# The output projection of attention: seven block products for each of three pairs of output blocks, with two sums of weight blocks formed by adding transfers

## The chip, the cores and the metric

The kernel runs on one core of a Trainium2 chip. The metric is the device time of one execution in microseconds (us); three runs of the kernel before gave 1672.11, 1672.30 and 1672.94, median 1672.3. The engines that matter here are PE (the matrix engine, with its weight loads PEld), DVE and ACT (the two elementwise engines), POOL (here: small scalings, a broadcast, and transfers of its own queue) and SP (which issues most transfers).

## The reference

A two-layer encoder on 512 tokens of width 1024. Each layer mixes tokens in three gated branches, projects the gated sum with `w_out`, adds it to the residual `x`, and then runs a gated convolutional feed-forward. The part that the change touches is `merged @ w_out` and the norm behind it:

```python
def gated_parallel_mixer(h, w_in, ...):
    ...
    merged = (gates[:, :, 0] * (y_na @ w_br_na)
              + gates[:, :, 1] * (y_mla @ w_br_mla)
              + gates[:, :, 2] * (y_gqa @ w_br_gqa))
    return merged @ w_out

def reference(x, ...):
    for l in range(DEPTH):
        h = rmsnorm(x, norm1_g[l])
        x = x + gated_parallel_mixer(h, ...)
        h = rmsnorm(x, norm2_g[l])
        x = x + conv_ffn(h, w_up[l], conv_w[l], conv_b[l], w_down[l])
    return rmsnorm(x, final_g)
```

## The kernel before, in words

Activations stand transposed: `x` is eight tiles of 128 channels by 512 tokens, and every projection takes weight blocks of 128x128 as the stationary operand and 512 (or 256) tokens as the moving one. All products are done in three passes: weight and activation are each split into a high and a low part (`split`, L195: ACT casts the high part at L198 or L201, DVE subtracts it from the source for the low part at L199 or L202), and `mm3` (L207) adds high x high, high x low, low x high.

Weights come in "specs" in one fixed list. For each, SP loads a `raw` tile (three buffers), ACT writes `whi` and DVE `wlo` (five buffers each), and `weights` (L186) hands them to the products. So a weight is split at the earliest when PE has done with the one five places before it. The order on PE and SP is that of the code (`manual_schedule`, L409); on DVE it is that of the code only inside the items named at L421, and elsewhere a scheduler picks one order when the kernel is built. Whatever the order, each engine runs its own list strictly in turn: a DVE instruction that waits holds up all behind it.

Near the end of attention `merge` (L793) forms `merged[m]` for eight output blocks and splits each into a pair of `mo` tiles. `do_out` (L929) then makes the eight output blocks: a group of four in two halves of the inner dimension, and four more of 24 matmuls each, 192 matmuls of 512 columns in all. As each block comes out (`evac`), DVE adds it to `x[k]`, and `norm_piece` splits `x[k]` times the gain into `hh`, `hl` and adds its square to `acc`.

`do_up` (L946) starts the feed-forward: a group of four output blocks, again in two halves (inner blocks 0 to 3, then 4 to 7; 48 matmuls each). After the second block of the first half PE transposes `acc` (L241), from which DVE, POOL, a transfer of the POOL queue and a POOL broadcast (L243 to L258) make `rb`, the inverse root mean square of each token. `conv` (L959) is the first to need `rb`: DVE multiplies each output by it into `u` (L962).

The feed-forward's last projection already uses seven products of half the tokens for a pair of output blocks instead of eight (`do_sum`, L1004, weight sums in `prepare_sum`, L168, activation sums in `operands`, L984): DVE adds four pairs of weight tiles per pair of output blocks, and `load_sum` (L153) loads their parts several products ahead. The group that follows it in layer 0 (`lat` of layer 1) has its `acc` transposed after the fourth block of its first half.

Of the kernel before, what the change touches and what calls it, by code (L numbers as in the profile page):

```python
# [17 lines left out]
P = 128  # L18
# [20 lines left out]
RAWB, WB, GZB, PRIO = 3, 3, 5, 300  # L39
NP, AHEAD, EVAC = (6, 5), (7, 7, 4, 7, 7, 7, 7), 400  # L40
F2 = 2 * NP[0]
# [22 lines left out]
class Trunk:  # L64
# [88 lines left out]
    def load_sum(self, j, unit):  # L153


        w = unit["np"] * P
        pool = self.fb if unit["part"] else self.fa
        for name in {0: ("V11", "V21", "V22"), 2: ("V12",)}.get(j, ()):
            m, e = unit["m"] + int(name[1]) - 1, int(name[2]) - 1
            if name in ("V11", "V22"):  # L160
                t = pool.tile([P, w], F32, tag="own", name="own", bufs=4)
# [4 lines left out]
            self.nc.sync.dma_start(unit[name].rearrange("p (i c) -> p i c", c=P), rows[e])  # L166

    def prepare_sum(self, hi, lo, j, unit):  # L168


        add, w = self.nc.vector.tensor_add, unit["np"] * P
        if j == 0:
            unit["S1"] = (self.fb if unit["part"] else self.fa).tile([P, w], F32, tag="s1", name="s1")
            unit["S2"], unit["S3"] = unit["S1"], unit["V21"]
            add(unit["S1"], unit["V21"], unit["V22"])
        elif j == 2:
            add(unit["S2"], unit["S1"], unit["V11"])
        elif j == 3:
            unit["S4"] = unit["V12"]
            add(unit["S4"], unit["S2"], unit["V12"])  # L180
        elif j == 5:
# [138 lines left out]
    def schedule(self, l):  # L320
# [33 lines left out]
        for part, ms in enumerate(((0, 2, 4, 6), (2, 4) if l == L - 1 else (2, 4, 6))):  # L354
            for m in ms:
                unit = {"w": d["w_down"][l], "m": m, "part": part, "np": NP[part], "r0": part * F2 * P}
                W["sum", part, m] = [("sum", j, unit) for j in range(7)]
# [23 lines left out]
        s += [("br", 2, 7)]  # L381
        s += ["out"] + [("out", m) for m in range(4, KD)]
        n = 2 * (F2 + 1)
# [4 lines left out]
    def run(self):  # L388
# [20 lines left out]
        with self.tc.manual_schedule(engines={mybir.EngineType.PE, mybir.EngineType.SP}):  # L409
# [3 lines left out]
            for self.l, (s, self.W) in enumerate(self.plans):  # L413
                self.pr = self.par[self.l]
                for item in s:
                    name, args = (item, ()) if isinstance(item, str) else (item[0], item[1:])
                    self.item = item
                    if name in ATTN:
                        with self.tc.high_priority(offset=ATTN_PRIO):
                            getattr(self, "do_" + name)(*args)  # L420
                    elif item == ("two", 0) or name == "sum" and args[0]:  # L421
                        with self.tc.manual_schedule(engines={mybir.EngineType.DVE}):
                            getattr(self, "do_" + name)(*args)
                    else:
                        getattr(self, "do_" + name)(*args)
# [367 lines left out]
    def merge(self, b, m, ps):  # L793
# [8 lines left out]
        if b == 2:  # L802
            if m == 0:
                self.gps_.close()
                self.ops, self.op = self.open("mo")
                self.mo = []
            pair = [self.op.tile([P, S], F32R, tag=f"{n}{m}", name="mo") for n in ("mh", "ml")]
            self.split(*pair, self.merged[m], 0.5)
            self.mo.append(pair)

# [117 lines left out]

    def do_out(self, m=None):  # L929
        g = self.pr[:, PC_G2:PC_G2 + 8]  # L930

        def evac(k, ps):
            if k == 0:
                self.norm_begin()
            self.nc.vector.tensor_add(self.x[k], self.x[k], ps)
            self.norm_piece(k, g)
        if m is None:
            self.banks(g=[2, 3, 4, 5], d=[6, 7, 0, 1])
            self.group(self.W["out"], self.mo, {(1, i): (lambda i=i: evac(i, self.gbank[i])) for i in range(4)})
        else:  # L940
            evac(m, self.dense(self.spec(), self.mo))
            if m == KD - 1:
                self.ops.close()
                self.mxs.close()
# [59 lines left out]
    def do_sum(self, part, m):  # L1004
# [8 lines left out]
        for j, (spec, (operand, b, x, sign)) in enumerate(zip(self.W["sum", part, m], steps)):  # L1013
            ps, fresh = banks[b], j in (0, 1, 2, 5)
            operand += part and operand > 0
            c = slice(operand * 256, operand * 256 + 256)
            for i, (wh, wl) in enumerate(self.weights(spec)):
# [3 lines left out]
                mm(ps, wl, hi, start=False, stop=i == n - 1, skip_group_check=True)  # L1021
            if part and j in (2,5):
                self.done(self.todo.pop(0))
            with self.tc.high_priority(offset=EVAC):
                if j < 6:
                    nc.vector.tensor_tensor(x, x, ps, ALU.add if sign > 0 else ALU.subtract)
                else:
                    both = x.rearrange("p (n c) -> p n c", c=256)
                    nc.vector.tensor_tensor(both, both, ps.rearrange("p (n c) -> p n c", n=1).to_broadcast([P, 2, 256]),
                                            ALU.subtract)  # L1030
        if part:
            self.todo += [m, m + 1]
            if m == KD - 2:
                self.done(m)
                self.done(m + 1)
        elif m == KD - 2:
# [4 lines left out]

    def done(self, k):
        if self.l == L - 1:
            self.acc = self.sumsq(self.const, self.x[k], self.acc, self.ntags)
# [4 lines left out]
        if k == KD - 1:  # L1049
            for i in range(KD):  # L1050
                self.acc = self.sumsq(self.const, self.x[i], self.acc, self.ntags)
            self.leave()

# [193 lines left out]
```

## Time and profile before

| what | us |
|---|---|
| median of three runs | 1672.3 |
| time of the profiled execution | 1673.28 |
| its span, first to last instruction | 1671.5 |
| PE busy (share of the span) | 1662.4 (99%) |
| DVE busy | 1270.6 (76%) |
| ACT busy | 895.6 (54%) |
| POOL busy | 50.8 (3%) |

The profiled execution is some 1 us longer than the median; 1.8 us of its time lie outside its span. A timeline row of the trace reads: start in us, duration in us, engine, line, operation, output<-input, shape, and in brackets how long the engine had stood idle before it and for what. Matmul durations overlap (each begins before the one ahead has drained), so the pace is read from the starts.

### The profile page before, as it was taken

The page shows a single profiled execution, that of the slowest core. Times are in us where ns is not written, and L with a number is a line of the kernel's source. Part 1 is how long each engine was busy: PE and PEld are TensorE (multiplying, and loading weights), DVE is VectorE, ACT ScalarE, POOL GpSimd, SP SyncE. Part 2 cuts the span into 40 slices and gives each one's busy share as a digit, 9 for nine tenths or more (in the row PEclk, how much of TensorE's full clock was granted, in tenths as well). Part 3 has the DMA queues.
Part 4 walks back from the last instruction along what each step waited for, and adds up shares of the span by engine and source line. Part 5 has one row for each costly group of instructions (what it writes and reads, how often), then busy time and mean ns, then how long its engine had stood idle before and what let it go on. Part 6 is the DMA issues. An engine that isn't in the chain of part 4 may idle for free.

```text
span 1671.5 us, 24066 instructions
## 1 busy us (share of the span) xinstructions
PE 1662.4 (99%) x9163; PEld 1405.3 (84%) x9163; DVE 1270.6 (76%) x2151; ACT 895.6 (54%) x1575; POOL 50.8 (3%) x107
## 2 busy tenths in 40 slices
PE   9999999999999999999999999999999999999998
PEld 7788888888888889888987888888888888898888
DVE  7777866787549888787977687668866588987886
ACT  7664545775436443445567544467744454434454
POOL 1110000000000000000011100000000000000000
PEclk9999999999999999999999999999999999999999
DMA  6233223222324333333233333322223333333322
GB/s 181 75 99 89 80 76 95 77 76 76 107 76 126 100 93 98 109 93 100 79 103 82 86 84 88 93 79 75 66 82 108 100 113 89 99 90 115 101 80 85
DMA packets 289667, 155.57 MB, mean 93 GB/s; under 512 B 9136, under 2 KB 285632, under 8 KB 289552
## 3 DMA queue, kind: packets, MB, share of 16 engines
q1 hardware_dynamic: 287008, 148.88, 31.3%
q0 software_dynamic: 2256, 4.83, 0.9%
q8 instruction: 72, 1.18, 0.3%
q14 instruction: 43, 0.35, 0.1%
q10 hardware_dynamic: 288, 0.33, 0.1%
HBM read 151.89 MB, written 2.10 MB: 92 GB/s over the span
## 4 chain that ended last, share of the span: by engine, by line
PE 92%; DVE 2%; ACT 1%; issue 0%; DMA 0%; ACTq 0%
PE ps_ring L212 12%; PE ps_ring L213 12%; PE ps_ring L214 12%; PE ps_d L214 11%; PE ps_d L212 11%; PE ps_d L213 11%; PE ps_d L1021 4%; PE ps_d L1020 4%; PE ps_d L1019 4%; PE ps_g L212 2%; PE ps_g L214 2%; PE ps_g L213 2%; PE ps_ring L293 2%; PE ps_ring L280 1%; PE ps_ring L762 1%; DVE wlo L199 1%
## 5 line engine op out<-in xcount | busy, mean ns | idle before, releaser
L198 ACT CAST whi<-raw 128x1024 fp32r<-128x1024 f32 (+5 forms) x342 | 293.7, 859 | 437.2 <-PE ps_ring L213 155.7
L199 DVE TENSOR_TENSOR wlo<-raw,whi 128x1024 fp32r<-128x1024 f32 (+5 forms) x340 | 335.5, 987 | 60.3 <-ACT whi L198 58.5
L214 PE MATMUL ps_d<-hh,wlo 128*128 128x512 f32 x685 | 266.7, 389 | 0.0
L212 PE MATMUL ps_d<-hh,whi 128*128 128x512 f32 x685 | 266.5, 389 | 0.0
L213 PE MATMUL ps_d<-hl,whi 128*128 128x512 f32 x685 | 266.5, 389 | 0.0
L212 PE MATMUL ps_ring<-hh,whi 128*128 128x512 f32 x600 | 235.3, 392 | 1.1 <-DVE nm L877 0.6
L214 PE MATMUL ps_ring<-hh,wlo 128*128 128x512 f32 x600 | 233.7, 390 | 0.0
L213 PE MATMUL ps_ring<-hl,whi 128*128 128x512 f32 x600 | 233.6, 389 | 0.0
L214 PEld LDWEIGHTS ps_d<-hh,wlo 128*128 128x128 f32 x685 | 128.6, 188 | 27.2 <-DVE wlo L199 0.6
L213 PEld LDWEIGHTS ps_d<-hl,whi 128*128 128x128 f32 x685 | 128.6, 188 | 26.8
L212 PEld LDWEIGHTS ps_d<-hh,whi 128*128 128x128 f32 x685 | 128.6, 188 | 26.5
L1021 PE MATMUL ps_d<-ft,wlo 128*128 128x256 f32 x511 | 144.6, 283 | 0.0
L1020 PE MATMUL ps_d<-ft,whi 128*128 128x256 f32 x511 | 144.6, 283 | 0.0
L1019 PE MATMUL ps_d<-ft,whi 128*128 128x256 f32 x511 | 144.6, 283 | 0.0
L212 PEld LDWEIGHTS ps_ring<-hh,whi 128*128 128x128 f32 x600 | 112.6, 188 | 25.4 <-DVE pt L734 0.9
L214 PEld LDWEIGHTS ps_ring<-hh,wlo 128*128 128x128 f32 x600 | 112.6, 188 | 23.7
L213 PEld LDWEIGHTS ps_ring<-hl,whi 128*128 128x128 f32 x600 | 112.7, 188 | 23.0
L1019 PEld LDWEIGHTS ps_d<-ft,whi 128*128 128x128 f32 x511 | 98.1, 192 | 0.2
L1020 PEld LDWEIGHTS ps_d<-ft,whi 128*128 128x128 f32 x511 | 98.1, 192 | 0.2
L1021 PEld LDWEIGHTS ps_d<-ft,wlo 128*128 128x128 f32 x511 | 98.1, 192 | 0.0
L205 DVE TENSOR_TENSOR gz<-ps_ring,rb 128x512 f32<-128x512 f32 x44 | 30.4, 690 | 77.0 <-PE ps_ring L214 77.0
L205 DVE TENSOR_TENSOR u<-ps_d,rb 128x512 f32<-128x512 f32 x80 | 54.9, 686 | 37.0 <-PE ps_d L214 36.7
(352 smaller groups left out, 3184.1 us busy)
## 6 DMA issues: line engine op xcount, KB each, us to landing
raw<-in_w_in_dram SPq DMA_DIRECT2D x86, 512.0 KB, 3.9
raw<-in_w_up_dram SPq DMA_DIRECT2D x80, 512.0 KB, 3.7
raw<-in_w_down_dram SPq DMA_DIRECT2D x18, 384.0 KB, 3.8
own<-in_w_down_dram SPq DMA_DIRECT2D x16, 384.0 KB, 4.9
raw<-in_w_in_dram SPq DMA_DIRECT2D x17, 256.0 KB, 3.0
raw<-in_w_br_mla_dram SPq DMA_DIRECT2D x16, 256.0 KB, 2.8
raw<-in_w_br_na_dram SPq DMA_DIRECT2D x16, 256.0 KB, 2.8
raw<-in_w_br_gqa_dram SPq DMA_DIRECT2D x16, 256.0 KB, 2.8
```

What stands on the lines that cost most here:

```text
L198: nc.scalar.copy(hi, src)
L199: nc.vector.tensor_sub(lo, src, r32(hi))
L205: self.nc.vector.tensor_tensor(out, a, b, ALU.mult)
L212: mm(ps, sh, mh, start=first and k == 0, stop=False)
L213: mm(ps, sh, ml, start=False, stop=False)
L214: mm(ps, sl, mh, start=False, stop=last and k == n - 1)
L280: self.nc.tensor.transpose(out[2 * u + i][:, c * 64:c * 64 + 64], block[q], self.idf[q, q])
L293: self.nc.tensor.matmul(out, st[a], mv[b], start=first and t == 0, stop=last and t == 2)
L762: nc.tensor.matmul(pq[:, qs], self.vs[p][:, ch, j, :], pm[:].rearrange("p (k c) -> p k c", c=P)[:, ks], start=i == 0 and m == 0, stop=i == ...
L1019: mm(ps, wh, hi, start=fresh and i == 0, stop=False, skip_group_check=True)
L1020: mm(ps, wh, lo, start=False, stop=False, skip_group_check=True)
L1021: mm(ps, wl, hi, start=False, stop=i == n - 1, skip_group_check=True)
```

## The change

`do_out` becomes one item. Output blocks 0 and 1 are made densely (four specs, 48 matmuls of 512 columns): both blocks over inner blocks 0 to 5 first, then both over 6 and 7. Blocks 2 to 7 are made as three pairs by `do_sum` with seven products of 4 inner pairs x 3 passes, 84 matmuls of 256 columns a pair.

- `merge` calls `mixed`, which splits `merged[m]` into a wider `mo` tile, and for each odd `m` also forms two sums of half-token blocks (four DVE operations of 256 columns) and splits them (two of 512 columns on ACT and on DVE). 
- `load_sum` loads the weight block V21 twice, and POOL's queue then adds V22 into the one copy and V11 into the other straight from DRAM (`accum_op=ALU.add`). These are S1 and S3, the second and the last of the seven weights. DVE adds only S2 and S4.
- The norm behind the projection: `done` (L1042 before) splits `x[k]` inside the following unit; the squares of all eight blocks are added to `acc` when the last block is done. In the last unit (blocks 6 and 7) of the projections that use it, the one of the feed-forward in layer 0 among them, the four `done` calls now stand at the second, fourth, sixth and seventh product.
- `do_up` transposes `acc` after the fourth block of the first half, where it was the second, and uses other PSUM banks.
- The items `out` and all `sum` of parts 1 and 2 now have DVE in the order of the code.

```diff
-NP, AHEAD, EVAC = (6, 5), (7, 7, 4, 7, 7, 7, 7), 400
+NP, AHEAD, EVAC = (6, 5, 4), (7, 7, 4, 7, 7, 7, 7), 400
...
+            unit["rows", name] = rows[e]
+        if j == 0 and unit["part"] == 2:
+            unit["S1"], unit["S3"] = self.mxt(f"ynl{self.owns // 2 % 2}"), unit["V21"]
+            view = lambda n: unit[n].rearrange("p (i c) -> p i c", c=P)
+            self.nc.sync.dma_start(view("S1"), unit["rows", "V21"])
+            for n, other in (("S1", "V22"), ("S3", "V11")):
+                self.nc.gpsimd.dma_start(view(n), unit["rows", other], accum_op=ALU.add)
...
-        W["out"] = halves(d["w_out"][l], [m * P for m in range(4)])
-        for m in range(4, KD):
-            W["out", m] = [(d["w_out"][l], 0, KD, m * P, P)]
+        W["out"] = [(d["w_out"][l], k0 * P, nk, m * P, P) for k0, nk in ((0, 6), (6, 2)) for m in (0, 1)]
...
-        s += ["out"] + [("out", m) for m in range(4, KD)]
+        s += ["out"] + [("sum", 2, m) for m in (2, 4, 6)]
...
-                    elif item == ("two", 0) or name == "sum" and args[0]:
+                    elif item in ("out", ("two", 0)) or name == "sum" and args[0]:
...
+    def mixed(self, m):
+        nc, (i, e) = self.nc, divmod(m, 2)
...
+        self.split(*part(e), self.merged[m], 0.5)
+        if e == 0:
+            return
+        (b0, b1), (b2, b3) = ((t[:, :256], t[:, 256:]) for t in self.merged[m - 1:m + 1])
+        a, t = self.mxt("ynl2"), self.mxt("ynl3")
+        nc.vector.tensor_sub(a[:, :256], b0, b1)
+        nc.vector.tensor_sub(a[:, 256:], b3, b1)
+        self.split(*part(2), a, 0.5)
+        nc.vector.scalar_tensor_tensor(t[:, :256], a[:, :256], -1.0, b3, ALU.mult, ALU.subtract)
+        nc.vector.scalar_tensor_tensor(t[:, 256:], t[:, :256], -1.0, b2, ALU.mult, ALU.subtract)
+        self.split(*part(3), t, 0.5)
...
-            self.banks(g=[2, 3, 4, 5], r=[6], d=[7, 0, 1, 2, 3, 4, 5, 6])
+            self.banks(g=[0, 1, 2, 3], r=[6], d=[7, 4, 5, 6, 0, 1, 2, 3])
...
-            self.group(self.W["up"], self.h, {(0, 1): lambda: (self.norm_sums(), self.norm_spread()), (1, 0): lambda: conv(0), (1, 1): lambda: conv(1),
+            self.group(self.W["up"], self.h, {(0, 3): lambda: (self.norm_sums(), self.norm_spread()), (1, 0): lambda: conv(0), (1, 1): lambda: conv(1),
...
-            if part and j in (2,5):
-                self.done(self.todo.pop(0))
+            if part and j in ((1, 3) if m == KD - 2 else (2, 5)):
+                self.done(self.todo.pop(0), part)
...
+            if part and m == KD - 2 and j > 4:
+                self.done(m + j - 5, part)
...
-    def done(self, k):
-        if self.l == L - 1:
+    def done(self, k, part=1):
+        if part == 2:
+            self.norm_split(k, self.pr[:, PC_G2:PC_G2 + 8])
+        elif self.l == L - 1:
```

Two places show what the change moves. The numbers behind the names tell one tile from the next. First PE in the first group of `do_up`, layer 0, before: `ps_g_4985` and `ps_g_4986` are the second and third output block, `ps_r` the transposed `acc`.

```order
L212 MATMUL ps_g_4985<-hh_4813,whi_4939 128x512
L213 MATMUL ps_g_4985<-hl_4814,whi_4939 128x512
L214 MATMUL ps_g_4985<-hh_4813,wlo_4940 128x512
L241 MATMUL ps_r_5024<-idf_78,acc_4740 128x128 x4
L212 MATMUL ps_g_4986<-hh_4736,whi_4990 128x512
L213 MATMUL ps_g_4986<-hl_4737,whi_4990 128x512
L214 MATMUL ps_g_4986<-hh_4736,wlo_4991 128x512
```

The same engine and place with the change (`ps_g_5238` is the fourth block, `ps_g_5235` the first):

```order
L232 MATMUL ps_g_5238<-hh_4976,wlo_5260 128x512
L230 MATMUL ps_g_5238<-hh_5031,whi_5259 128x512
L231 MATMUL ps_g_5238<-hl_5032,whi_5259 128x512
L232 MATMUL ps_g_5238<-hh_5031,wlo_5260 128x512
L259 MATMUL ps_r_5311<-idf_78,acc_5203 128x128 x4
L230 MATMUL ps_g_5235<-hh_5097,whi_5277 128x512
L231 MATMUL ps_g_5235<-hl_5098,whi_5277 128x512
```

The transposes moved back by two blocks, 24 matmuls: they stand between the two halves of the group now.

Second, DVE from the reduction of that transposed `acc` to the first weight behind the group (its `wlo` is 1024 wide: `wlo_5132` before), before the change. `u` is an output of the group times `rb`, `c` a step of the convolution; the 512-wide `wlo` are weights of the group's second half.

```order
L243 TENSOR_REDUCE ms_5029<-ps_r_5024 128x4
L199 TENSOR_TENSOR wlo_5041<-raw_5038,whi_5040 128x512
L199 TENSOR_TENSOR wlo_5059<-raw_5056,whi_5058 128x512
L199 TENSOR_TENSOR wlo_5077<-raw_5074,whi_5076 128x512
L205 TENSOR_TENSOR u_5092<-ps_g_4984,rb_5034 128x512
L199 TENSOR_TENSOR wlo_5101<-raw_5098,whi_5100 128x512
L966 SCALAR_TENSOR_TENSOR c_5094<-u_5092,x0_67,c_5094 128x511
L967 SCALAR_TENSOR_TENSOR c_5094<-u_5092,x0_67,c_5094 128x511
L205 TENSOR_TENSOR u_5116<-ps_g_4985,rb_5034 128x512
L199 TENSOR_TENSOR wlo_5132<-raw_5129,whi_5131 128x1024
```

With the change, the same stretch of DVE (`wlo_5383` is the first weight behind the group, `wlo_5407` the next):

```order
L261 TENSOR_REDUCE ms_5316<-ps_r_5311 128x4
L217 TENSOR_TENSOR wlo_5328<-raw_5325,whi_5327 128x512
L217 TENSOR_TENSOR wlo_5352<-raw_5349,whi_5351 128x512
L223 TENSOR_TENSOR u_5343<-ps_g_5235,rb_5321 128x512
L223 TENSOR_TENSOR u_5367<-ps_g_5236,rb_5321 128x512
L217 TENSOR_TENSOR wlo_5383<-raw_5380,whi_5382 128x1024
L994 SCALAR_TENSOR_TENSOR c_5345<-u_5343,x0_67,c_5345 128x511
L994 SCALAR_TENSOR_TENSOR c_5369<-u_5367,x0_67,c_5369 128x511
L995 SCALAR_TENSOR_TENSOR c_5345<-u_5343,x0_67,c_5345 128x511
L217 TENSOR_TENSOR wlo_5407<-raw_5404,whi_5406 128x1024
```

Two more of the group's 512-wide weights stand ahead of the reduction now, and between the first `u` and the first weight behind the group there is one instruction (the second `u`) where there were four; that weight still stands behind the first `u`. Layer 1 has the same order at both places.

More of the change, by code (lines that the diff above doesn't have):

```diff
@@ L160, in load_sum @@
             if name in ("V11", "V22"):
-                t = pool.tile([P, w], F32, tag="own", name="own", bufs=4)
+                t = self.own(unit["part"], w)
             else:
@@ L166, in load_sum, with sums, own @@
             self.nc.sync.dma_start(unit[name].rearrange("p (i c) -> p i c", c=P), rows[e])
+            unit["rows", name] = rows[e]
[5 more added lines that the diff above has]
+                self.nc.gpsimd.dma_start(view(n), unit["rows", other], accum_op=ALU.add)
+    def sums(self, part):
+        return self.fb if part else self.fa
+    def own(self, part, w):
+        if part < 2:
+            return self.sums(part).tile([P, w], F32, tag="own", name="own", bufs=4)
+        self.owns += 1
+        return self.mxt(f"ynh{self.owns % 4}")
     def prepare_sum(self, hi, lo, j, unit):
         add, w = self.nc.vector.tensor_add, unit["np"] * P
-        if j == 0:
-            unit["S1"] = (self.fb if unit["part"] else self.fa).tile([P, w], F32, tag="s1", name="s1")
+        loaded = unit["part"] == 2
+        if j == 0 and loaded:
+            unit["S2"] = unit["S1"]
+        elif j == 0:
+            unit["S1"] = self.sums(unit["part"]).tile([P, w], F32, tag="s1", name="s1")
             unit["S2"], unit["S3"] = unit["S1"], unit["V21"]
@@ L180, in prepare_sum @@
             add(unit["S4"], unit["S2"], unit["V12"])
-        elif j == 5:
+        elif j == 5 and not loaded:
             add(unit["S3"], unit["V11"], unit["V21"])
@@ L805, in merge @@
                 self.ops, self.op = self.open("mo")
[L806 to L809, printed above, removed]
+                self.ff, self.owns = [], 0
+            self.mixed(m)
+    def mixed(self, m):
+        nc, (i, e) = self.nc, divmod(m, 2)
+        if e == 0:
+            self.ff.append([self.op.tile([P, 8 * 256], F32R, tag=f"m{n}{i}", name="mo") for n in "hl"])
+        part = lambda a: [t[:, a * S:(a + 1) * S] for t in self.ff[i]]
+        self.split(*part(e), self.merged[m], 0.5)
+        if e == 0:
+            return
[7 more added lines that the diff above has]
+        self.split(*part(3), t, 0.5)
     def do_gq_open(self):
@@ L1014, in do_sum @@
             ps, fresh = banks[b], j in (0, 1, 2, 5)
-            operand += part and operand > 0
+            operand += part > 0 and operand > 0
             c = slice(operand * 256, operand * 256 + 256)
@@ L1051, in done @@
                 self.acc = self.sumsq(self.const, self.x[i], self.acc, self.ntags)
-            self.leave()
+            if part == 2:
+                self.ops.close()
+                self.mxs.close()
+            else:
+                self.leave()
     def leave(self):
```

36 lines of the change are left out of this document (15 added, 21 removed).

## Prediction

> **What bounds the kernel now.** First the page's head, engine shares and chain of waits:
>
> ```profile
> span 1671.5 us, 24066 instructions
> PE 1662.4 (99%) x9163; PEld 1405.3 (84%) x9163; DVE 1270.6 (76%) x2151; ACT 895.6 (54%) x1575; POOL 50.8 (3%) x107
> PE 92%; DVE 2%; ACT 1%; issue 0%; DMA 0%; ACTq 0%
> ```
>
> PE holds 99% of the span and 92% of the chain. So what the change saves in PE time counts in full, and every wait it puts in front of PE counts in full too. Next the table by windows: the kernel's first 8 us, the last merges of layer 0, its output projection, and a stretch of seven-product units. Behind the window stand busy time and count of PE, PEld, DVE, ACT, POOL, then the granted clock, the DMA share and GB/s.
>
> ```profile
> 0.00:8.00 8.00, 6.54 (x26) 5.38 (x26) 3.04 (x10) 3.75 (x6) 0.40 (x5) 1.00 0.75 237
> 395.00:437.50 42.50, 42.50 (x189) 35.13 (x189) 26.49 (x42) 16.66 (x26) 0.00 (x0) 1.00 0.31 87
> 437.50:481.00 43.50, 43.50 (x194) 36.02 (x192) 25.54 (x36) 18.46 (x28) 0.00 (x0) 1.00 0.37 103
> 623.00:683.00 60.00, 60.00 (x501) 59.92 (x500) 51.47 (x75) 25.04 (x30) 0.00 (x0) 1.00 0.31 86
> ```
>
> PE never stands still in the stage that is rewritten, at full clock; DVE works 26.5 of 42.5 us before it and 25.5 of 43.5 in it. The timeline of PE gives the pace, and the places I need later:
>
> ```profile
> 1.04 3.35 PE L412 MATMUL idle<-early 128*128 128x128 f32 x14 [1.04 <-DVE cst L89]
> ...
> 437.70 0.39 PE L212 MATMUL ps_g<-mo,whi 128*128 128x512 f32 x1
> ...
> 481.00 0.39 PE L214 MATMUL ps_d<-mo,wlo 128*128 128x512 f32 x1
> 481.23 0.39 PE L212 MATMUL ps_g<-hh,whi 128*128 128x512 f32 x1
> ...
> 486.67 0.60 PE L241 MATMUL ps_r<-idf,acc 128*128 128x128 f32 x4
> ...
> 503.45 0.39 PE L212 MATMUL ps_d<-hh,whi 128*128 128x512 f32 x1
> 503.68 0.39 PE L213 MATMUL ps_d<-hl,whi 128*128 128x512 f32 x1
> 503.95 0.50 PE L214 MATMUL ps_d<-hh,wlo 128*128 128x512 f32 x1
> 504.29 0.39 PE L212 MATMUL ps_d<-hh,whi 128*128 128x512 f32 x1
> ...
> 623.31 0.28 PE L1019 MATMUL ps_d<-ft,whi 128*128 128x256 f32 x1
> ...
> 683.78 0.40 PE L212 MATMUL ps_d<-hh,whi 128*128 128x512 f32 x1
> ```
>
> The projection's 192 matmuls of 512 columns run from 437.70 to 481.23: 0.2267 us each. Four units of 126 matmuls of 256 columns run from 623.31 to 683.78: 0.1200 us each, a little over half.
>
> **The change, part by part.**
>
> *PE work.* Per layer 192 x 0.2267 = 43.5 us become 48 x 0.2267 + 252 x 0.1200 = 10.9 + 30.2 = 41.1 us: 2.4 us saved, 4.8 in two layers. The trace holds both paces side by side, so this term is firm. The Trainium skill ("TensorE: Matmul & The Clock Gate", section on the back-to-back issue gap) has 518 cycles at 2.4 GHz for 512 columns and 262 for 256, an estimate of 0.216 and 0.109 us; with those the saving would be 144 x 0.216 - 252 x 0.109 = 3.6 us a layer, 7.3 in all. The rows have a relatively dearer 256-column matmul, and the rows decide.
>
> *The norm behind the projection.* This is where I expect the saving to go. The timelines of DVE and POOL from the transposes of `acc` on, with the same `u` in layer 1 and the transposes ahead of it:
>
> ```profile
> 487.31 0.69 DVE L243 TENSOR_REDUCE ms<-ps_r 128x4 f32<-128x512 f32 x1 [2.04 <-PE ps_r L241]
> ...
> 499.05 0.69 DVE L205 TENSOR_TENSOR u<-ps_g,rb 128x512 f32<-128x512 f32 x1 [5.16 <-POOL rb L258]
> ...
> 502.08 0.68 DVE L205 TENSOR_TENSOR u<-ps_g,rb 128x512 f32<-128x512 f32 x1
> 502.68 1.21 DVE L199 TENSOR_TENSOR wlo<-raw,whi 128x1024 fp32r<-128x1024 f32 x1
> ```
>
> ```profile
> 490.25 0.74 POOL L257 DMA_DIRECT2D row<-rt  x1 [0.45 <-POOL rt L248]
> 497.81 1.21 POOL L258 PARTITION_BROADCAST rb<-row  x1 [6.81 <-issue]
> ```
>
> ```profile
> 1313.41 0.60 PE L241 MATMUL ps_r<-idf,acc 128*128 128x128 f32 x4
> ...
> 1325.77 0.69 DVE L205 TENSOR_TENSOR u<-ps_g,rb 128x512 f32<-128x512 f32 x1 [5.14 <-POOL rb L258]
> ```
>
> From the transposes to the first `u` it is 12.38 us in layer 0 and 12.36 in layer 1, most of it between POOL's transfer and its broadcast. Call the transposes' start T. Before, T comes 5.44 us after the group's start (486.67 - 481.23), the group ends 22.22 us after its start (503.45), and the first weight behind it is ready just in time: its subtraction starts at 502.68, and the matmul that needs it at 503.95, 0.05 late and with 0.11 us lost to the restart (504.29 - 503.95 = 0.34 in place of 0.23).
>
> With the change T lies 48 x 0.2267 = 10.88 us after the start. PE then needs 0.46 us for the transposes and 48 matmuls for the second half, and reaches the first matmul with the next weight's low part at T + 0.46 + 10.88 + 0.45 = T + 11.79. DVE's order has both `u` ahead of that weight: first `u` at T + 12.38, second 0.60 later (502.68 - 502.08), the subtraction at T + 13.58, the matmul 1.27 us after that (503.95 - 502.68), T + 14.85. PE waits 3.06 us, and pays 0.11 for the restart; 0.16 of that it paid before. Loss: 3.0 us a layer, 6.0 in all. Behind the waiting `u` on DVE stand this weight and all later ones. The next weight, after three steps of `c` of about 0.7, is done some 3.3 us after the first and is needed 5.4 us after it, so I count one wait a layer.
>
> *Is `acc` itself in time?* PE runs in order, so a late `acc` would delay it directly. The end of the feed-forward in layer 0 has the same pattern already (last unit, eight squares, transposes after the fourth block), on DVE and PE:
>
> ```profile
> 833.33 0.69 DVE L1029 TENSOR_TENSOR x<-x,ps_d 128x512 f32<-128x512 f32 x1 [0.53 <-PE ps_d L1021]
> 833.93 0.75 DVE L202 SCALAR_TENSOR_TENSOR hl<-x,par,hh 128x512 fp32r<-128x512 f32 x1
> 834.59 0.68 DVE L199 TENSOR_TENSOR wlo<-raw,whi 128x512 fp32r<-128x512 f32 x1
> ...
> 839.95 2.27 DVE L231 TENSOR_TENSOR acc<-acc,sq 128x512 f32<-128x512 f32 x3
> ```
>
> ```profile
> 844.04 0.60 PE L241 MATMUL ps_r<-idf,acc 128*128 128x128 f32 x4
> ```
>
> There `acc` is done at 842.2, 1.8 us before PE asks. The change has one more weight split ahead of the last addition, 0.6 us: 1.2 us of cover. I count nothing.
>
> *DVE in the seven-product units.* A unit of 84 matmuls lasts 10.08 us on PE. The evacuations of 256 columns on DVE's timeline, each with the row behind it:
>
> ```profile
> 797.61 0.41 DVE L1026 TENSOR_TENSOR x<-x,ps_d 128x256 f32<-128x256 f32 x1
> 797.94 0.82 DVE L180 TENSOR_TENSOR raw<-s,raw 128x640 f32<-128x640 f32 x1
> ...
> 799.41 0.41 DVE L1026 TENSOR_TENSOR x<-x,ps_d 128x256 f32<-128x256 f32 x1
> 799.81 0.83 DVE L199 TENSOR_TENSOR wlo<-raw,whi 128x640 fp32r<-128x640 f32 x1
> ```
>
> They take 0.33 and 0.40, mean 0.36. DVE does 7 weight splits and 2 additions of 512 columns (0.60 each by the spacing of the two rows at 502), six such evacuations and one of 512, and two norm splits of 0.66 (834.59 - 833.93): 5.4 + 2.2 + 0.6 + 1.3 = 9.5 us. With the two additions that the transfers take over it would be 10.7, more than PE. In the last unit, with three norm splits, it is 10.2; the five weight buffers carry 0.1 us. Nothing counted; 0.5 us a unit, 3 in all, as the other end.
>
> *The half-token sums in* `mixed`*.* Per pair of blocks four DVE operations of 256 and two of 512, 4 x 0.33 + 2 x 0.60 = 2.5 us. Three pairs fall among the last merges, where DVE stood idle for 16 us, and one at the projection's head, where it stood idle for 18 us of the whole; ACT is idle longer still. Hidden; without that cover it would be 2.5 us a pair.
>
> *The adding transfers.* No row before shows one. The nearest are in the listing of transfers by line, with size and median time to landing, and on SP's timeline:
>
> ```profile
> own<-in_w_down_dram SPq DMA_DIRECT2D x16, 384.0 KB, 4.9
> raw<-in_w_out_dram SPq DMA_DIRECT2D x16, 256.0 KB, 2.8
> rope<-in_rope_dram POOLq DMA_DIRECT2D x6, 256.0 KB, 3.4
> rope<-in_rope_dram SPq DMA_DIRECT2D x2, 256.0 KB, 7.0
> ```
>
> ```profile
> 804.68 0.53 SPq L166 DMA_DIRECT2D own<-in_w_down_dram  x1
> ```
>
> The low end is 3.4 us (the same queue and bytes, without adding), the high end 7.0 (twice the data, or the slowest transfer of this size); I take 3.4, the same queue. What hides it: the third pair's tiles can be loaded when DVE has split the first pair's S3, by an estimate from the five buffers when PE is at that pair's sixth product. From there to the third pair's second product it is ten products of 1.44 us, less 1.3 for the two steps of its own split: 13.1 us. The way is 3 x 0.5 (issues on SP) + 4.9 (loads, queued behind each other) + 2 x 0.74 (POOL's issues, by its row above) + 3.4 = 11.3, or 14.9 by the high end: 1.8 us of cover, or 1.8 late. The first pair's tile waits for a raw buffer that comes free with the last merge but one, 2.7 us before the projection begins, and is needed 12.3 us into it: about the same. DVE stands in turn behind a late S1, and PE behind it. Nothing counted; 1.8 us at each of two places, 3.6 a layer, 7.2 in all, as the other end. A gain from these transfers beyond the additions they replace is excluded, since PE waits for no such sum here.
>
> **The sum.** -4.8 + 6.0 = +1.2 us. The profiled execution's 1673.28 would become 1674.5; on the median of the runs, 1672.3, it is 1673.5. A measurement of this kernel can tell about 0.2%, 3.3 us, from no change.
>
> **The rivals.**
>
> *The saving arrives whole* (faster): the chain from T to `rb` shortens, or the next weight's split is not behind it. Then 1672.3 - 4.8 = 1667.5. Against it: two layers agree on the chain within 0.02 us, and DVE's order is fixed. Chance 0.09.
>
> *The adding transfers land late* (slower). Place: the splits of S1 in the first and third pair. It decides once a transfer takes more than 5.2 us from its issue (3.4 + 1.8). At the high end of 7.0 it costs 7.2 us, and the time is 1673.5 + 7.2 = 1680.7. For it: nothing in the trace bounds an adding transfer. Against it: SP's queue moves the same pieces of this weight in 2.8 us. Chance 0.12, half of it below 1678.
>
> *PE comes back slow after the wait* (slower). If it ran at half pace for as long as it had stood still, 3.1 us a layer, 6.2 in all: 1679.7. The same page of the Trainium skill (its part on the clock gate) says that PE falls to half its clock after an idle window of about 3.4 us. No row here shows a fallen clock: the longest wait in the timeline above is the 1.04 us at the start, and the first 8 us show 1.00. The forecast's wait is just under the page's window. Chance 0.07.
>
> *DVE becomes the bound in the units, or* `acc` *is late*: up to 3 us in all, 1674 to 1677. Chance 0.10.
>
> **How the numbers follow.** The forecast, one wait of 2.5 to 3.5 us a layer, 1672.5 to 1674.5, has 0.62, and the likeliest time is 1673.5. The range takes in the late `acc`, the transfers up to 5 us of their 7.2, and the case of a full DVE, 1671.0 to 1678.5; left out are the whole saving (0.09) and the far slower ends (about 0.09). Faster than 1669.0 is the first rival, 0.09; slower than 1675.6 are the late transfers (0.12), the slow PE (0.07) and half of the last case (0.05), 0.24; the rest, 0.67, is no measurable change.
>
> **What would show it.** Right: the profile after has PE idle about 3 us, at the third matmul of the first block behind the group of `do_up`, once a layer, put down to DVE's `wlo` behind `u` behind POOL's `rb`; the three units take 10.1 us each with no idle time on PE. Wrong: no such wait, or waits at the second product of a unit put down to a transfer on POOL's queue, or units longer than 10.3 us with DVE full.

## The result, and the profile after

The changed kernel takes 1691.7 us (median of four executions, 1688.9 to 1693.5), the kernel before 1672.3 beside it: a ratio of 1.0114, 95% interval 1.0097 to 1.0132. It is slower by 19 us, where 1.2 was forecast and 1678.5 was the range's upper end. The profiled execution took 1688.92 us, the shortest of the four; the other three had a mean granted clock of 0.994 or 0.995, this one 0.996, so what follows accounts for the shortest of them. Its page has, in answer to the three lines of before:

```profile
span 1687.1 us, 24783 instructions
PE 1666.2 (99%) x9379; PEld 1416.9 (84%) x9379; DVE 1315.8 (78%) x2267; ACT 915.3 (54%) x1617; POOL 68.3 (4%) x119
PE 65%; DVE 1%; issue 1%; DMA 1%; ACT 0%; POOLq 0%; POOL 0%; SPq 0%; ACTq 0%
```

PE still shows 99%, and is busy for longer although it has less to do: busy time says little where the clock falls. The chain of waits is no better guide here: PE's share of the span in it fell from 92% to 65%, but the chain, followed back from the end, stops at 507.84 us, at the first `u`, where before it went back to 63.51; the two shares cover different stretches. To see where the 15.6 us of span went, cut both traces at the same four instructions: first matmul of the projection, first of the feed-forward's group, the same two in layer 1, and the end. The columns are those of the table by windows (third from the end: the granted clock). Before:

```profile
437.70:481.23 43.53, 43.53 (x194) 36.04 (x193) 25.54 (x36) 18.29 (x29) 0.00 (x0) 1.00 0.37 103
481.23:1264.44 783.21, 782.10 (x4366) 662.49 (x4365) 606.75 (x1028) 424.54 (x749) 24.68 (x49) 1.00 0.32 91
1264.44:1307.96 43.52, 43.52 (x193) 36.05 (x192) 25.54 (x36) 18.28 (x29) 0.00 (x0) 1.00 0.36 103
1307.96:1671.50 363.54, 358.38 (x1975) 313.25 (x1973) 290.64 (x427) 173.34 (x237) 3.58 (x4) 1.00 0.33 98
```

After:

```profile
436.64:484.59 47.95, 44.17 (x302) 41.12 (x300) 35.70 (x68) 22.44 (x39) 7.79 (x6) 0.96 0.59 124
484.59:1272.17 787.58, 783.86 (x4368) 663.70 (x4366) 619.59 (x1055) 430.11 (x760) 24.71 (x49) 1.00 0.33 91
1272.17:1318.33 46.16, 43.63 (x302) 39.93 (x300) 35.34 (x68) 22.56 (x39) 7.78 (x6) 1.00 0.62 129
1318.33:1687.10 368.77, 360.02 (x1976) 314.32 (x1974) 295.54 (x435) 175.78 (x242) 3.56 (x4) 0.99 0.34 99
```

The two projections grew by 4.4 and 2.6 us, where 2.4 less was reckoned for each; the two stretches behind them grew by 4.4 and 5.2, where 3.0 was reckoned. (The sum is 16.7; 1.1 comes back because the first projection began 1.1 us earlier here.) What PE waited for, in us in all, times and the longest:

```profile
PE ps_d L232 <- DVE wlo L217: 5.7, 2, 2.9
PE ps_d L1047 <- ACT whi L216: 4.8, 3, 2.6
PE ps_d L1049 <- DVE wlo L217: 1.1, 5, 0.2
```

The first row is the forecast's wait for `rb`, once a layer. DVE's timeline in layer 0 has its cause, `u` waiting for `rb` and the weight standing behind both `u`:

```profile
507.86 1.29 DVE L223 TENSOR_TENSOR u<-ps_g,rb 128x512 f32<-128x512 f32 x2 [7.86 <-POOL rb L276]
509.07 1.22 DVE L217 TENSOR_TENSOR wlo<-raw,whi 128x1024 fp32r<-128x1024 f32 x1
```

The second is the one that the forecast named as the sign of its being wrong: PE stands ahead of a unit's second product, whose weight is S1. PE's timeline at the first pair of layer 0:

```profile
448.83 0.28 PE L1049 MATMUL ps_d<-mo,wlo 128*128 128x256 f32 x1
451.73 0.39 PE L1047 MATMUL ps_d<-mo,whi 128*128 128x256 f32 x1 [2.62 <-ACT whi L216]
...
452.92 0.41 PE L1049 MATMUL ps_d<-mo,wlo 128*128 128x256 f32 x1
453.13 0.41 PE L1047 MATMUL ps_d<-mo,whi 128*128 128x256 f32 x1
```

Behind the wait the matmuls start 0.21 us apart in place of 0.12. The table by windows shows why, around this wait and around the one for `rb` in both layers:

```profile
448.80:452.90 4.10, 1.25 (x8) 0.84 (x7) 1.19 (x2) 1.84 (x4) 1.28 (x1) 1.00 0.10 11
452.90:456.40 3.50, 3.50 (x19) 3.50 (x18) 3.50 (x8) 2.70 (x5) 0.16 (x1) 0.51 0.60 75
...
507.00:510.40 3.40, 0.52 (x4) 0.10 (x2) 2.54 (x4) 1.81 (x3) 0.83 (x1) 1.00 0.00 0
510.40:514.50 4.10, 4.10 (x11) 3.24 (x12) 4.10 (x6) 1.95 (x3) 0.00 (x0) 0.58 0.44 128
...
1344.10:1347.70 3.60, 3.60 (x10) 2.83 (x11) 3.60 (x6) 1.59 (x2) 0.00 (x0) 0.57 0.50 146
```

The granted clock is half for some 3.5 us behind each wait of 2.6 us or more, and it is 1.00 behind the one of 1.5 us at S1 in layer 1. Why S1 is late, from the timelines of POOL and ACT and the listing of transfers (the last number is the median time to landing):

```profile
439.63 1.39 POOL L172 DMA_DIRECT2D raw<-in_w_out_dram  x1 [238.54 <-DMA ynh<-in_w_out_dram]
445.13 1.29 POOL L172 DMA_DIRECT2D ynl<-in_w_out_dram  x1 [4.11 <-DMA raw<-in_w_out_dram]
451.29 1.28 POOL L172 DMA_DIRECT2D raw<-in_w_out_dram  x1 [4.87 <-issue]
456.24 1.27 POOL L172 DMA_DIRECT2D ynl<-in_w_out_dram  x1 [3.67 <-issue]
```

```profile
451.06 0.62 ACT L216 CAST whi<-ynl 128x512 fp32r<-128x512 f32 x1 [5.62 <-DMA ynl<-in_w_out_dram]
```

```profile
raw<-in_w_out_dram POOLq DMA_DIRECT2D x6, 256.0 KB, 4.6
ynl<-in_w_out_dram POOLq DMA_DIRECT2D x6, 256.0 KB, 5.4
```

POOL issues S3's adding transfer (into `raw`) ahead of S1's (into `ynl`) in every pair, although the code lists S1 first; an issue takes 1.3 us, and where the next stands ready it goes out 4.7 to 6.2 us after the one ahead, mostly with nothing to wait for that the profile shows ("issue"). The first pair's S1 came out at 445.13, its sum was there at 451.06, and PE had needed the split weight by about 448.95.

### The profile page after: what moved, and what is told of

Same layout as the page of the kernel before. It is cut to its first block, busy times and chain, and to the rows that moved or that the text cites. A ratio compares the mean times of both kernels' runs of the same rounds, so it can differ in the third digit from the quotient of the medians.

```text
span 1687.1 us, 24783 instructions
## 1 busy us (share of the span) xinstructions
PE 1666.2 (99%) x9379; PEld 1416.9 (84%) x9379; DVE 1315.8 (78%) x2267; ACT 915.3 (54%) x1617; POOL 68.3 (4%) x119
## 4 chain that ended last, share of the span: by engine, by line
PE 65%; DVE 1%; issue 1%; DMA 1%; ACT 0%; POOLq 0%; POOL 0%; SPq 0%; ACTq 0%
PE ps_d L232 10%; PE ps_d L231 10%; PE ps_d L230 10%; PE ps_ring L230 6%; PE ps_ring L231 6%; PE ps_ring L232 6%; PE ps_d L1049 4%; PE ps_d L1048 4%; PE ps_d L1047 4%; DMA ynl<-in_w_out_dram 1%; PE ps_ring L311 1%; PE ps_g L230 1%; PE ps_g L232 1%; PE ps_g L231 1%; PE ps_ring L298 1%
## 5 line engine op out<-in xcount | busy, mean ns | idle before, releaser
L216 ACT CAST whi<-raw 128x1024 fp32r<-128x1024 f32 (+4 forms) x344 | 291.2, 847 | 402.1 <-PE ps_ring L231 140.0
L217 DVE TENSOR_TENSOR wlo<-raw,whi 128x1024 fp32r<-128x1024 f32 (+4 forms) x342 | 331.6, 970 | 40.9 <-ACT whi L216 39.5
```

The source lines that it names most:

```text
L216: nc.scalar.copy(hi, src)
L217: nc.vector.tensor_sub(lo, src, r32(hi))
```

## The experiments

The theory: three losses, S1 late because of the adding transfers, the wait for `rb`, and half the clock behind each long wait. The rivals: another cause for the slow stretches, DVE full in the units, or transfers that are slow wherever they stand. Beside all of these kernels the kernel before took 1672.1 to 1672.3 us (and 1672.9 in the one execution beside the two probes of POOL).

### The weights behind the group ahead of `u` on DVE

```diff
+            with self.tc.manual_schedule(engines={mybir.EngineType.DVE}):
+                self.group(self.W["up"], self.h, {(0, 3): ..., (1, 3): lambda: conv(0)})
+            conv(1, 2, 3)
```

> The changed kernel, but in the first group of the feed-forward DVE splits both weights behind the group ahead of the first u, so that no weight stands behind rb. Theory (the wait for rb of 2.9 us a layer, and behind it some 3.5 us in which PE is granted about half its clock, 1.6 to 1.9 us lost each time): both go, 2 x (3.0 + 1.7) = 9.4 us less than the changed kernel's 1691.7, so 1682. Rival A (the slow stretch has another cause than the wait, such as the transfers of that time): only the waits go, 1685.7. Rival B (the next thing that depends on rb, a PSUM bank or the third weight behind the group, is late in its turn): 1688 to 1692.

1683.1 us (1681.2 to 1684.2), ratio 1.0065 (1.0051 to 1.0079): 8.6 less than the changed kernel. DVE's timeline now has both weights ahead of `u`, and PE no wait there and full clock:

```profile
502.26 1.23 DVE L217 TENSOR_TENSOR wlo<-raw,whi 128x1024 fp32r<-128x1024 f32 x1 [2.46 <-ACT whi L216]
504.98 1.23 DVE L217 TENSOR_TENSOR wlo<-raw,whi 128x1024 fp32r<-128x1024 f32 x1 [1.49 <-ACT whi L216]
507.58 1.29 DVE L223 TENSOR_TENSOR u<-ps_g,rb 128x512 f32<-128x512 f32 x2 [1.37 <-POOL rb L276]
```

```profile
502.00:510.00 8.00, 8.00 (x37) 6.63 (x36) 4.87 (x6) 3.86 (x5) 1.22 (x1) 1.00 0.57 166
```

`rb` is as late as ever and nobody waits for it but `u`. The loss was a matter of one queue's order, and the slow stretch went with the wait: rivals A and B fall.

### The transposes alone, in the kernel before

```diff
-{(0, 1): lambda: (self.norm_sums(), self.norm_spread()), ...
+{(0, 3): lambda: (self.norm_sums(), self.norm_spread()), ...
```

> The kernel before, with one edit: the transposes of acc after the fourth block of the first half instead of the second. The dense projection stays, and no adding transfer is in it. Theory: the wait for rb and the slow stretch behind it appear here too, 2 x (3.0 + 1.7) = 9.4 us over 1672.3, so 1681.7, with a granted clock of 0.5 to 0.6 for some 3.5 us behind each wait. Rival A (the clock falls for another reason, in the new units or their transfers): 1672.3 + 6.0 = 1678.3 with the clock at 1.00.

1682.2 us, ratio 1.0055 (1.0040 to 1.0070): as the theory had it, without one new unit or adding transfer. The slow stretch is not in every execution to the same amount: the four took 1683.9, 1683.3, 1681.2 and 1679.2 us, at mean granted clocks of 0.996, 0.996, 0.997 and 0.999. The profile is of the longest. Behind the waits:

```profile
507.20:512.00 4.80, 4.58 (x13) 3.63 (x14) 4.80 (x8) 2.65 (x3) 0.00 (x0) 0.64 0.42 122
...
1338.50:1345.50 7.00, 7.00 (x19) 5.51 (x20) 7.00 (x10) 4.58 (x7) 0.00 (x0) 0.57 0.51 150
```

In layer 1 the low clock lasted about 6 of these 7 us, nearly twice the 3.4 us of layer 0, behind the shorter of the two waits (2.9 us, and 3.7 in layer 0).

### S1's transfers first

```diff
+        if j == 0 and unit["part"] == 2:
+            unit["S1"] = self.mxt(...)
+            self.nc.sync.dma_start(view("S1"), rows(unit["m"] + 1, 0))
+            self.nc.gpsimd.dma_start(view("S1"), rows(unit["m"] + 1, 1), accum_op=ALU.add)
         for name in {0: ("V11", "V21", "V22"), 2: ("V12",)}.get(j, ()):
...
+            unit["S3"] = unit["V21"]
+            self.nc.gpsimd.dma_start(view("S3"), rows(unit["m"], 0), accum_op=ALU.add)
```

> The changed kernel, but S1's plain load and its adding transfer are issued ahead of the other loads of their unit, on SP and on POOL; S3's adding transfer stands behind S1's. Theory (S1 comes late because POOL issues S3's transfer first and each takes 1.3 us to issue and 4.4 to 5.9 to land): S1 is there 5 us earlier, the waits at the second product go in both layers (2.8 + 0.8 and 1.7 us), with the slow stretch behind the longest (1.7), so 7 us less than 1691.7: 1685. Rival A (the units wait because DVE is full, or because the transfers are slow as such wherever they stand): 1689 to 1692. Rival B: S3 is late now, the last product waits: 1688 to 1692.

1677.7 us, ratio 1.0035 (1.0021 to 1.0049). The cause is confirmed, and its price was put too low: 14 us less, not 7. The projections take 42.15 and 41.11 us here in place of 47.95 and 46.16, so besides the longest waits went the short ones (0.1 to 0.4 us each) behind them, which I had left out: by the starts of PE's matmuls they make up 3.3 of the 5.05 us that layer 1's projection loses in the changed kernel, and S1's wait only 1.7. The waits for `rb` are still there, 2.8 us in layer 0 and 2.5 in layer 1, and what follows them is telling:

```profile
505.00:509.00 4.00, 3.84 (x17) 3.17 (x18) 4.00 (x7) 1.85 (x3) 0.00 (x0) 1.00 0.45 131
...
1332.00:1337.00 5.00, 5.00 (x15) 3.96 (x16) 5.00 (x8) 2.85 (x3) 0.00 (x0) 0.66 0.51 151
```

The longer wait was followed by a full clock, the shorter by half of it for about 3.4 of the 5 us. So the stretch from the group of layer 0 to the next projection prices the wait alone: 785.98 us here, against 782.85 where no wait is left (the last kernel below), 3.1 us. With the slow stretch, in the changed kernel, it was 787.58: 1.6 us for the clock.

### Both edits

> The changed kernel with both edits, the two weights ahead of the first u and S1's transfers first. Theory: every loss over 1 us is gone and the saving in PE work of 4.8 us is left, 1667.5; with the gaps of about 1 us in the second and third pair still there, up to 1672. Rival (the units are bound by DVE, or the seven products cost more on PE than their pace in the feed-forward says): 1674 to 1678.

1668.8 us, ratio 0.9979 (0.9971 to 0.9988). The two edits save 8.6 and 14.0 us, and together 22.9. No wait of PE over 1.0 us is left, and that one is at the start. Its projections take 42.00 and 41.12 us.

### The wait for `rb` filled with matmuls

```diff
+            idle, (wh, _) = self.bank("r"), self.parts[self.used - 1]
+            for _ in range(13):
+                self.nc.tensor.matmul(idle, wh[:, 0, :], self.h[0][0], start=True, stop=True)
```

> The kernel with S1's transfers first (1677.7 us), and between the group of the feed-forward and the first weight behind it 13 more matmuls of 512 columns into a bank that nobody reads, 13 x 0.227 = 2.95 us a layer, as long as PE waits there. The wait is filled, not shortened: the weight comes as late as before. Theory (behind an idle stretch of 2.8 us or more PE gets half its clock, not in every execution): the granted clock stays at 1.00, and the time is that of the kernel with both edits and two waits, 1668.8 + 2 x 2.9 = 1674.6. Rival (the slow stretch comes from the transfers or from DVE's pace at that time): 1677.7 or, since the fill may be longer than the wait, up to 1678.2.

1675.3 us (1674.2 to 1676.1), ratio 1.0018 (1.0009 to 1.0027): 2.4 less than with the wait (every execution is below the shortest there, 1676.6), though PE got 2.95 us more to do in each layer. The window behind the fill in layer 0 (layer 1 has 1.00 there too):

```profile
504.00:508.00 4.00, 4.00 (x19) 3.17 (x18) 4.00 (x6) 2.01 (x3) 0.00 (x0) 1.00 0.40 114
```

DVE and the transfers do then what they did before, the weight comes as late, and the clock stays full. So it is the idle time of PE that brings the clock down, not what the other engines do meanwhile. The edit is that of the kernel with S1 first plus these lines, and so is the next.

### Four matmuls of fill

> The same with 4 matmuls, 0.9 us, so that PE still stands idle for about 1.9 us. Theory (a wait of 1.7 us was followed by no slow stretch, those of 2.8 us and more mostly were): clock at 1.00, 1674.6. Rival (any wait of about 2 us brings the clock down): 1677.7, with 0.5 to 0.6 granted behind both waits.

1677.1 us (1674.1 to 1678.5), ratio 1.0027 (1.0018 to 1.0037): the rival's number. But the profiled execution was the fastest of nine, 1674.1, and shows waits of up to 2.2 us and a full clock behind them:

```profile
PE ps_d L233 <- DVE wlo L218: 4.1, 2, 2.2
```

Its executions spread over 4.4 us, those with the wait filled over 1.9. That fits a clock that falls behind a wait of 2 us in some executions and not in others. That it can is seen in the first experiment, at S1 of layer 0 (PE's timeline, and the window behind it):

```profile
450.65 0.38 PE L1048 MATMUL ps_d<-mo,whi 128*128 128x256 f32 x1 [2.01 <-ACT whi L216]
```

```profile
450.60:455.00 4.40, 4.13 (x21) 3.93 (x22) 4.37 (x9) 3.93 (x7) 0.90 (x2) 0.61 0.48 60
```

The theory's line between 1.7 and 2.8 us does not hold: from about 2 us on the length of the wait alone does not decide it, and what does is not shown.

### Plain transfers in place of adding ones

```diff
-                self.nc.gpsimd.dma_start(view(n), unit["rows", other], accum_op=ALU.add)
+                self.nc.gpsimd.dma_start(view(n), unit["rows", other])
```

> The changed kernel, but POOL's six transfers a pair of layers write V22 and V11 over S1 and S3 instead of adding them; pieces, queue and order stay. It leaves the two weight sums out. Theory (the price is the adding: 1.3 us to issue and 5 us to land, one at a time, where the plain ones of that queue take 0.55 and 3.3): S1 lands about 4 us earlier, no wait at the second products, about 14 us less, 1678. Rival (the price is POOL's queue with pieces of 512 bytes, adding or not): the same waits, 1690 to 1693.

This kernel leaves the two sums out, so only its times mean something. 1677.2 us, ratio 1.0027 (1.0017 to 1.0037), no wait at the second products. POOL's timeline and the listing:

```profile
439.37 0.77 POOL L172 DMA_DIRECT2D raw<-in_w_out_dram  x1 [238.68 <-DMA ynh<-in_w_out_dram]
441.24 0.76 POOL L172 DMA_DIRECT2D ynl<-in_w_out_dram  x1 [1.10 <-PE ps_d L232]
```

```profile
raw<-in_w_out_dram POOLq DMA_DIRECT2D x6, 256.0 KB, 3.4
ynl<-in_w_out_dram POOLq DMA_DIRECT2D x6, 256.0 KB, 3.7
```

Issues of 0.76 us and landings of 3.4 and 3.7: these are the very prices of the forecast, 0.74 and 3.4. They were right for a plain transfer and wrong for an adding one. And S1's goes out 1.9 us behind S3's, where the adding one took 5.5 us, although its own load has to land first here too: that load was not what held it.

### DVE forms all four sums

The kernel with the weights ahead of `u`, no adding transfer, and `add` for S1 and S3 as in the feed-forward.

> The kernel with both weights ahead of the first u, and without any adding transfer: DVE adds S1 and S3 as it does in the feed-forward, 10.7 us of DVE in units of 10.08 by the prediction's count. Theory (DVE is the bound then): 0.6 us a unit, six units, over the 1668.8 of the kernel with both edits: 1672.4. Rival (DVE has the slack, as it stood idle ahead of the units): 1668 to 1669, and the adding transfers bring nothing. Other end (a late sum in each unit, with waits of 1 us): 1676.

1668.7 us, ratio 0.9978 (0.9969 to 0.9987): the rival. The projection of layer 0 (that of layer 1 takes 41.73 us):

```profile
436.17:477.89 41.72, 41.72 (x301) 39.48 (x300) 38.88 (x75) 22.72 (x39) 0.00 (x0) 1.00 0.31 84
```

DVE works 38.9 of 41.7 us and PE never stops. The stage is 0.6 us longer than at its best; the forecast's 10.7 against 10.08 us a unit would have made it 1.8 longer. So the adding transfers can save 0.6 us a layer at most, and as whole transfers in a good order (1668.8) they saved nothing.

### Two probes of POOL's queue

A memset on POOL behind each adding transfer, and each of them cut in two:

```diff
+                self.nc.gpsimd.memset(self.small.tile([P, 4], F32, ...), 0.0)
```

```diff
+            for i in (0, 2):
+                self.nc.gpsimd.dma_start(view("S1")[:, i:i + 2], rows(unit["m"] + 1, 1)[:, i:i + 2], accum_op=ALU.add)
```

> The kernel with both edits (1668.8 us), and on POOL a small memset of 128x4 right behind each adding transfer. It tells what is held for some 3.7 us behind each of them, when the profile shows nothing that POOL waits for. Theory A (POOL itself is held until the adding transfer is nearly done): the memset starts 3.4 to 5 us after the end of the issue. Theory B (only the queue takes one adding transfer at a time): the memset starts within 0.3 us of the issue's end, and the next transfer still 4.7 to 5 us after the one ahead of it. Time 1668 to 1670 either way.

> The kernel with both edits, each adding transfer cut into two of 128 KB. Theory A (the 5 us from one adding transfer to the next grow with its pieces): two halves go at 2.5 us each, issues of 0.65 us, and the six sums are formed in the same time, 1668 to 1670. Theory B (a fixed price for each transfer, whatever its size): 4 to 5 us for each half, 9 us for a sum, POOL needs 18 us for the two sums of a unit of 10 us, the third pair's S1 comes late by about 10 us: 1685 to 1700.

One execution of each: 1668.3 and 1666.6 us. POOL's timeline with the memset:

```profile
444.55 1.30 POOL L176 DMA_DIRECT2D raw<-in_w_out_dram  x1 [5.37 <-issue]
445.33 0.63 POOL L177 MEMSET pr<- 128x4 f32 x1
449.74 1.28 POOL L163 DMA_DIRECT2D ynl<-in_w_out_dram  x1 [3.79 <-issue]
```

The memset starts while the issue still shows, and the next transfer starts 5.2 us after the one ahead: what is held is not POOL but its next transfer, theory B. With halves:

```profile
436.90 2.54 POOL L163 DMA_DIRECT2D ynl<-in_w_out_dram  x2 [236.22 <-DVE ynl L839]
439.91 1.20 POOL L175 DMA_DIRECT2D raw<-in_w_out_dram  x1 [0.47 <-DVE ynl L842]
442.49 1.19 POOL L175 DMA_DIRECT2D raw<-in_w_out_dram  x1 [1.38 <-issue]
```

The first two go out back to back, 1.27 us each, and the gaps ahead of the next two are 0.5 and 1.4 us. Neither a price that grows with the pieces (2.5 us a half) nor a fixed one (4 to 5) fits all of that: in these traces the gap of 3.4 us and more, with nothing shown to wait for, stands behind adding transfers of 512 pieces alone. What it is stays open.

### Halves as the only edit

> The changed kernel with one edit: each adding transfer cut into two of 128 KB; S3's still go ahead of S1's, and the weight behind the group still stands behind u. Theory (what made S1 late is that POOL puts out nothing for 3.5 us and more behind an adding transfer of 512 pieces, and does not do so with 256 pieces: the two halves of S3 then take about 2.5 us ahead of S1 instead of 5.5): S1's second half is issued some 2 us earlier than the whole one was, the waits at the second products shrink from 2.8 us to 1 us or less, the slow stretch behind them goes, and what is left is near the kernel with S1 first, 1677.7 (1676 to 1680). Rival (the halves need as long as the whole): 1690 to 1693.

1683.2 us, ratio 1.0063 (1.0049 to 1.0077): between the theory's 1676 to 1680 and the rival. Of three waits for S1 two are left:

```profile
PE ps_d L1048 <- ACT whi L217: 3.7, 2, 2.4
```

In layer 0 S1's second half goes out at 443.83, 1.3 us earlier than the whole one did and not 2, since S3's two halves, 2.5 us together, still go first and begin at 439.30. Cutting the transfer helps, and the order matters more.

### Both edits with halves

> The kernel with both edits and halved adding transfers once more, timed in rounds. Theory (no wait is left for the halves to shorten; its one time of 1666.6 lies within what executions differ by): 1667.5 to 1668.8, as with whole transfers. Rival (whole transfers still cost about 1 us a layer in short gaps of the units): 1666.6.

1667.3 us (1666.8 to 1668.0), ratio 0.9970 (0.9958 to 0.9981): 5.0 us under the kernel before, the best of all. Its stages:

```profile
436.87:477.98 41.11, 41.11 (x302) 39.24 (x300) 36.09 (x69) 22.99 (x39) 14.60 (x12) 1.00 0.69 144
477.98:1260.83 782.85, 782.00 (x4367) 662.47 (x4366) 619.00 (x1055) 429.59 (x759) 24.84 (x49) 1.00 0.32 92
1260.83:1301.94 41.11, 41.11 (x301) 39.23 (x300) 36.09 (x69) 22.98 (x39) 14.60 (x12) 1.00 0.69 143
1301.94:1665.40 363.46, 358.25 (x1976) 313.30 (x1974) 295.30 (x435) 175.31 (x241) 3.58 (x4) 1.00 0.34 100
```

That lies between theory and rival: whole transfers cost 0.9 us in the first layer's projection (42.00) and nothing in the second's (41.12).

## Why the prediction was wrong, step by step

Set against this last kernel, in which the change does what it can, the changed kernel's profiled execution loses 6.84 and 5.05 us in the projections and 4.7 and 5.3 us behind them. Of the 5.3 us, 0.7 are no part of it: the end of the span comes 5.1 us after the issue of the last output transfer, where it is 4.4 in the last kernel and 4.3 in the kernel before.

*PE work, 41.1 us a layer: right.* 41.11 us, twice. The saving of 4.8 us is real: it gives 1667.5, and the last kernel took 1667.3.

*The wait for* `rb`*, 3.0 us a layer: right,* in place, cause and size. It was 2.9 us, 3.1 with its restart.

*PE's pace behind the wait: a rival at 0.07, and it happened,* in both layers and once more behind S1's wait, at about 1.6 us each where 3.1 was reckoned. The step that failed is the condition. I set the wait of 3 us against an idle window of 3.4 and called it just under. The Trainium skill ("TensorE: Matmul & The Clock Gate", section on what's actually happening) gives that window and adds that it runs freely, which I did not use; if PE must stand still for one whole window, a wait shorter than that leaves the clock alone. The traces do not agree: in the profiles of the kernels above that stood still long enough, the clock fell behind 10 of the 13 waits of 2.4 to 3.7 us, all three of the changed kernel's among them, behind one of three of 2.0 to 2.2 us, and behind none shorter than that. By windows of half a microsecond the low clock lasted 3.4 us in nine of these eleven cases, 3.1 in one and 6.0 in one. The measurement decides.

*The adding transfers, counted at nothing: the step that failed,* and the largest, 11.9 us in the two projections. "I take 3.4, the same queue" set a plain transfer's price for an operation that no row showed. Measured: 1.3 us to issue in place of 0.74, 4.6 and 5.4 to land (medians), and then 3.4 us or more in which the queue puts out nothing. From the load of the first pair's V21 on SP (435.8) to S1's sum it was 15.3 us, where 11.3 was reckoned and 14.9 with the high end. Term by term: the loads took 3.8 us in place of 6.4, the step from one adding transfer to the next 5.5 in place of 0.74, and S1's own 5.9 in place of 4.1. The term that failed most is the one between the two transfers. I had also left out that POOL's order may put S3 first, which is what lays these 5.5 us on S1, and had priced a late transfer as its own lateness (1.8 us a place), without the shorter waits behind it and the clock. Of the rival at 0.12 the places were right (S1 of the first pair in both layers, 2.6 and 1.5 us, and of the third in layer 0, 0.6). Its mechanism, a slow landing, was the smaller part, and its price of 7.2 was too low.

*DVE in the units, nothing counted: right,* and its rival is weaker than thought: even with all four sums on DVE it cost 0.6 us a layer.

*`acc` in time, `mixed` hidden: right.* No wait shows at either.

One error of the text ahead: weights have three buffers, not five (`RAWB, WB, GZB, PRIO = 3, 3, 5, 300`), so a weight is split when PE has done with the one three places before. The estimate of when the third pair's tiles can be loaded, at the first pair's sixth product, was drawn from the wrong number, and so was the 0.1 us that five buffers were to carry in the last unit; no run singles these out.

The sum, made again with what was measured against the kernel before: -4.8 for the work, +11.9 for S1 and what follows it, +8.85 for the waits for `rb` with their slow stretches and +0.75 for the later end of the last transfer (9.6 together, 4.37 + 5.23 by the windows), -1.1 for the earlier start: +15.6, the difference of the two spans.

## What to carry to other kernels

Ask of each operation that the profile does not show what it holds up behind it, not only how long it takes; here the hold behind an adding transfer, 5.5 us where 0.74 was reckoned, was the larger error. Let the bound that decides the sign into the forecast's own range. A reduction that moves later is best followed along the queue of the engine that consumes it: here two weights moved ahead of one waiting instruction were worth 8.6 us. And where a wait on the bounding engine reaches 2 us, price what its clock does behind it, too.

## What was not expected of the hardware

An adding transfer of 512 pieces of 512 bytes kept the next one on POOL's queue back for some 5 us from its start, while POOL itself went on; plain ones followed each other in 1.3 to 2.0 us within a pair, adding ones of 256 pieces mostly in 1.2 to 2.6. PE's clock fell to half behind waits from 2.0 us up, mostly for 3.4 us, but not always: a wait of 3.2 us was followed by full clock (halves as the only edit, layer 0: 1.00 from 508.11 to 512.00), one of 2.0 us by half.
